# Other cost figures in the planner that orders the side work of a one-core decoder block

## The chip, the cores and the metric

The kernel runs on one core of a Trainium2 chip. Its time is the device time of one execution in microseconds (us); the figure given is the median of several. The core has five engines that each take their own instructions in order: TensorE (PE, matrix multiplication), VectorE (DVE), ScalarE (ACT), GpSimd (POOL) and SyncE (SP), which here only issues transfers.

## The reference

One layer of a hybrid decoder block on 256 rows of width 2048, all in float32. A normed input goes through one wide projection (17 slices); three branches mix the rows (a gated linear recurrence, sparse attention with compressed, selected and window keys, and attention with a forget bias); each is gated, projected, scaled by a merge gate and summed; an output projection, and an embedding that is gated by another projection, are added.

```python
hn = rms_norm(h, ln_gain[l])
z = split_columns(hn @ w_in[l] + b_in[l])
y_a = rglru_branch(z['lru_x'], ...) * jax.nn.silu(z['lru_gate'])
...
y_b = nsa_branch(q_b, k_c, v_c, k_s, v_s, k_w, v_w, g_b) * jax.nn.silu(z['nsa_gate'])
y_c = fox_branch(...) * jax.nn.silu(z['fox_gate'])
merged = (mg[:, :, 0] * (y_a @ w_branch[l, 0])
          + mg[:, :, 1] * (y_b @ w_branch[l, 1])
          + mg[:, :, 2] * (y_c @ w_branch[l, 2]))
h = h + merged @ w_out[l]
e = rms_norm(p[l] @ w_ple[l], ple_gain[l])
h = h + jax.nn.sigmoid(h @ w_ple_gate[l]) * e
```

## The kernel before, in words

**Main work.** All weights are one stream of 384 pieces of up to 128 x 1024 values ("halves" in the code; called pieces here). SP loads a piece into one of six `raw` tiles. ACT rounds it to the fast matmul type (`wh<-raw`), DVE subtracts to get the remainder (`wl<-raw,wh`), and PE multiplies with both: three matmuls of 128x512 for each product, so that the result is near float32. A usual piece has two rows of 128 weights and two row blocks (t) of the output, which makes 12 matmuls. `wh` and `wl` each have four buffers (`AHEAD`+1, line 1391): the rounding of a piece waits until PE is done with the piece four places earlier. Results grow in `main0` to `main3`, two at a time, in turns.

**The order of the stream.** Input slices first, among them `nsa_gate`; then for each of the three branches b and four column groups j one `merge` group (eight pieces, the merge gate) and one `proj` group (four pieces, the branch's projection); then output and embedding gate. "Proj 0" below is the first projection of branch A; "merge 0" is the group ahead of it, and "merge 1" the one behind. Proj 0 reads `yh` and `yl`, the two parts of branch A's gated output `yl` (the name `k_yl` stands for both the branch output and the low part).

**Side work.** Everything else is written as generators that are advanced a step at a time between the pieces: `lru_task` (line 741; four of them, lru0 to lru3, two channel tiles each, of branch A: convolution, gates, a scan into `yl`), `nsa_task` (line 922; eight, of branch B: scores in a `bank`, a maximum, an exponential with row sums, scaling, a turn through a transposition and DMAs, the product with V), `fox_task` (branch C), `norm_rows`, `turn_chunk` and so on. `y_split` (line 1102) waits for all four lru tasks; it multiplies by the gate (`k_yl<-k_yl,k_gl`), rounds (`k_yh<-k_yl` on ACT) and subtracts (`k_yl<-k_yl,k_yh` on DVE), in four steps of two channel tiles.

**What sets the order.** While the program is built, a planner keeps a clock for each engine. Each recorded instruction passes through `Metered.run` (line 207; all instructions therefore carry line 208 in the profile), which adds an estimated cost to its engine's clock; `Clock.add` lets it start only after what it reads. `Side.tick` (line 257) is called once or twice a piece and advances up to three waiting tasks in turn, but returns as soon as the later of the DVE and ACT clocks is more than `LIMITS` (2.5 to 3.5 us, line 1404) ahead of PE's clock. Urgent tasks (`turn_chunk`, `norm_rows`, `y_split`) are advanced ahead of the others. `settle`, `powers` and `landed` hold a task until PE's clock has passed a moment, so that PE's small matmuls stand behind enough main work. `need` (line 1281) is the other end: where a piece cannot be written until a task is done (each `proj` piece needs one step of `y_split`), it advances tasks without regard to the limit until it is:

```python
for name in wait:
    n = 0
    while name not in side.done:
        ...
        clock.t["pe"] += 200.0
        side.tick(True)
```

These clocks exist only while the program is built. On the chip each engine simply runs its list, with semaphores.

## Time and profile before

| | |
|---|---|
| median of 3 runs | 1060.82 us (1060.35 to 1060.99) |
| profiled execution, its time | 1061.77 us |
| its span from first to last instruction | 1060.0 us |
| PE busy | 1053.3 us, 99% of the span |
| PE weight loads busy | 879.3 us, 83% |
| DVE busy | 772.2 us, 73% |
| ACT busy | 620.6 us, 59% |
| DMA moved | 237.52 MB, mean 224 GB/s |

### The profile page before, as it was taken

What the parts mean: (1) busy time and instruction counts of PE and PEld (TensorE: products, weight loads), DVE (VectorE), ACT (ScalarE), POOL (GpSimd) and SP (SyncE); (2) the same over time, 40 slices, a digit from 0 to 9 for tenths busy, and PEclk for the clock granted to TensorE, in tenths of its full rate; (3) what the DMA queues carried; (4) which work ended last, traced back from release to release, by engine and by line L of the source; (5) the groups of instructions that cost most, each with busy time, mean ns of one, the idle gap of its engine ahead of it and who ended that gap; (6) DMA issues with size and microseconds to landing.
All of it is one profiled execution on the core that took longest, in us unless ns stands there. A gap on an engine that the chain in (4) does not pass through costs nothing.

```text
span 1060.0 us, 14061 instructions
## 1 busy us (share of the span) xinstructions
PE 1053.3 (99%) x4903; PEld 879.3 (83%) x4903; DVE 772.2 (73%) x1151; ACT 620.6 (59%) x940; POOL 53.1 (5%) x77
## 2 busy tenths in 40 slices
PE   9999999999999999999999999999999999999998
PEld 7888889888888888888888888888888888888886
DVE  7777889897778678678987965555766566766664
ACT  7668877768766667544645644555555444444442
POOL 0000001110000000020110000000001000000000
PEclk9999999999999999999999999999999999999999
DMA  9767868787657467577677566766676877778751
GB/s 337 248 201 260 257 200 280 233 266 226 217 189 218 150 198 216 182 234 251 194 235 239 186 222 207 223 213 214 219 244 196 264 235 220 236 250 257 278 207 60
DMA packets 86295, 237.52 MB, mean 224 GB/s; under 512 B 14024, under 2 KB 31312, under 8 KB 86224
## 3 DMA queue, kind: packets, MB, share of 16 engines
q1 hardware_dynamic: 81504, 220.87, 64.8%
q0 software_dynamic: 4720, 15.76, 5.5%
q8 instruction: 38, 0.62, 0.3%
q14 instruction: 33, 0.27, 0.1%
HBM read 215.61 MB, written 4.20 MB: 207 GB/s over the span
## 4 chain that ended last, share of the span: by engine, by line
PE 91%; DVE 3%; DMA 2%; ACT 2%; SPq 1%; issue 1%; DVEq 0%; ACTq 0%
PE main L208 87%; PE bank L208 4%; SPq L208 1%; DVE wl L208 1%; DMA raw<-in_w 1%; DMA k_fpz<-k_fprob 1%; DMA k_pz<-k_prob 1%; ACT wh L208 0%; ACT k_pz L208 0%; DVE k_fq L208 0%; DVE k_prob L208 0%; DVE k_fprob L208 0%; DVE k_pt L208 0%; DVE k_fbias L208 0%; DVE k_fx L208 0%
## 5 line engine op out<-in xcount | busy, mean ns | idle before, releaser
L208 DVE TENSOR_TENSOR wl<-raw,wh 128x1024 fp32r<-128x1024 f32 (+2 forms) x388 | 459.8, 1197 | 186.0 <-ACT wh L208 185.2
L208 ACT ACTIVATE wh<-raw 128x1024 fp32r<-128x1024 f32 (+2 forms) x388 | 400.2, 1040 | 318.3 <-PE main L208 281.3
L208 PE MATMUL main<-wh,k_hnh 128*128 128x512 f32 (+2 forms) x1026 | 395.0, 385 | 0.5 <-ACT wh L208 0.5
L208 PE MATMUL main<-wh,k_hnl 128*128 128x512 f32 (+1 forms) x1024 | 393.0, 384 | 0.0
L208 PE MATMUL main<-wl,k_hnh 128*128 128x512 f32 (+2 forms) x1026 | 392.9, 384 | 0.0
L208 PEld LDWEIGHTS main<-wh,k_hnh 128*128 128x128 f32 x1026 | 193.2, 189 | 37.5 <-ACT wh L208 1.1
L208 PEld LDWEIGHTS main<-wh,k_hnl 128*128 128x128 f32 x1024 | 192.5, 188 | 38.1
L208 PEld LDWEIGHTS main<-wl,k_hnh 128*128 128x128 f32 x1026 | 193.2, 189 | 35.9 <-DVE wl L208 0.2
L208 PE MATMUL main<-wl,k_yh 128*128 128x512 f32 x192 | 74.9, 390 | 0.1
L208 PE MATMUL main<-wh,k_yh 128*128 128x512 f32 x192 | 74.9, 390 | 0.0
L208 PE MATMUL main<-wh,k_yl 128*128 128x512 f32 x192 | 74.8, 389 | 0.0
L208 PE MATMUL main<-wh,k_mth 128*128 128x512 f32 x128 | 49.8, 389 | 0.0
L208 PE MATMUL main<-wl,k_mth 128*128 128x512 f32 x128 | 49.8, 389 | 0.0
L208 PE MATMUL main<-wh,k_mtl 128*128 128x512 f32 x128 | 49.8, 389 | 0.0
L208 PE MATMUL main<-wh,k_hth 128*128 128x512 f32 x128 | 49.8, 389 | 0.0
L208 PE MATMUL main<-wl,k_hth 128*128 128x512 f32 x128 | 49.8, 389 | 0.0
L208 PE MATMUL main<-wh,k_htl 128*128 128x512 f32 x128 | 49.8, 389 | 0.0
L208 PEld LDWEIGHTS main<-wl,k_yh 128*128 128x128 f32 x192 | 36.0, 188 | 7.7 <-DVE wl L208 0.5
L208 PEld LDWEIGHTS main<-wh,k_yl 128*128 128x128 f32 x192 | 36.0, 188 | 7.5
L208 PEld LDWEIGHTS main<-wh,k_yh 128*128 128x128 f32 x192 | 36.1, 188 | 7.4
L208 ACT ACTIVATE k_mg<-k_mg 128x512 f32<-128x512 f32 x24 | 15.2, 633 | 26.6 <-DVE k_mg L208 26.3
L208 PEld LDWEIGHTS main<-wl,k_mth 128*128 128x128 f32 x128 | 24.0, 188 | 5.0
(243 smaller groups left out, 948.4 us busy)
## 6 DMA issues: line engine op xcount, KB each, us to landing
raw<-in_w SPq DMA_DIRECT2D x369, 512.0 KB, 4.5
bias<-in_b_in POOLq DMA_DIRECT2D x21, 256.0 KB, 5.2
raw<-in_w SPq DMA_DIRECT2D x8, 408.0 KB, 4.0
k_pz<-k_prob SPq DMA_DIRECT2D x16, 128.0 KB, 4.2
e_dram<-k_e POOLq DMA_DIRECT2D x4, 512.0 KB, 3.6
k_merged<-k_zt SPq DMA_DIRECT2D x16, 128.0 KB, 3.2
k_xc<-in_x POOLq DMA_DIRECT2D x4, 512.0 KB, 6.4
k_hx<-k_zt SPq DMA_DIRECT2D x16, 128.0 KB, 3.6
```

The costliest lines, as they stand in the source:

```text
L208: r = call(out, *args, **kw)
```

## The change

The planner's estimates for three kinds of instruction become larger; no tile, no instruction and no limit is changed by hand.

```diff
                 cost = 185.0 + 93.0 * columns + 0.833 * n + (1280.0 if tables != clock.tables else 0.0)
+                if "accum_out" in kw and n >= P:
+                    cost += n
                 clock.tables = tables
             elif which == "v":
-                cost = 150.0 + 1.05 * n
+                if name == "tensor_reduce":
+                    n = 1
+                    for m in ins[0].shape[1:]:
+                        n *= m
+                spaced = any(x.ap[-1][0] != 1 and x.shape[-1] > 1 for x in [out] + ins)
+                cost = 150.0 + (1.7 if spaced or name == "tensor_tensor_scan" else 1.05) * n
```

So an ACT instruction that also sums its rows is charged one nanosecond more for each element of a row, a DVE row reduction is charged by what it reads in place of what it writes, and DVE instructions with an operand whose elements do not lie side by side, and scans, are charged 1.7 ns an element in place of 1.05.

With other estimates the planner writes the same instructions in another order: each engine has as many as before, ACT changes its function table nine times in both, and the lists of PE, DVE and ACT part where the first lru tasks begin, in the first input slices. Three places are shown here, around the start of proj 0.

**DVE, the last scan of branch A (`k_yl<-k_lru`, the end of lru3).** Before, it stands among the remainders (`wl`) of merge 0's early pieces, and the gated products follow long after:

```order
L208 SCALAR_TENSOR_TENSOR k_lru_2527<-k_uc_2209,k_lru_2527 128x512
L208 TENSOR_TENSOR k_lru_2527<-k_lru_2527,k_lru_2526 128x512
L208 TENSOR_TENSOR wl_2606<-raw_2490,wh_2605 128x1024
L208 TENSOR_TENSOR wl_2630<-raw_2532,wh_2629 128x1024
L208 SCALAR_TENSOR_TENSOR k_yl_567<-k_lru_2525,k_lru_2527 128x256 x2
L208 TENSOR_TENSOR wl_2648<-raw_2559,wh_2647 128x1024
```

Now it stands behind the two `k_mg<-main` rows, which read merge 0's finished result, and the first gated product (`k_gl`) and its low part (`k_yh`) come a softmax later:

```order
L208 SCALAR_TENSOR_TENSOR k_mg_2953<-main_85,rsr,bias_2814 128x512
L208 SCALAR_TENSOR_TENSOR k_mg_2954<-main_86,rsr,bias_2814 128x512
L208 SCALAR_TENSOR_TENSOR k_yl_567<-k_lru_2699,k_lru_2701 128x256 x2
L208 ISA sp_pc_2742,sp_m_2740<-bank_87,cst 128x16
L208 ISA k_prob_2744,sp_m_2740<-bank_88,cst 128x256
L208 ISA k_prob_2744,sp_m_2740<-bank_87,cst 128x256
L208 TENSOR_SCALAR sp_sm_2729<-sp_sm_2729 128x6
L208 SCALAR_TENSOR_TENSOR k_pc_472_2731<-sp_pc_2730,sp_sm_2729,k_pc_472_2731 128x2x16
L208 STREAM_TRANSPOSE k_prob_2732<-k_pz_2733 128x512
L208 TENSOR_TENSOR k_ql_2994<-k_qn_2101,k_qh_2993 128x256
L208 TENSOR_TENSOR k_yl_567<-k_yl_567,k_gl_982 128x512
L208 TENSOR_TENSOR k_yl_2998<-k_yl_567,k_yh_2997 128x512
```

(Of the softmax the rows that repeat are left out: six ISA rows in all, a reciprocal and a product on `sp_sm`, a second `k_pc` and two pairs of `k_pz` scalings.)

**ACT at the same place, now.** Between merge 0's tanh (`k_mg`) and the first `k_yh` stand a rounding of a weight piece, the exponentials of two heads, their `k_pc` parts and the next query's `k_qh`:

```order
L208 ACTIVATE wh_2934<-raw_2841 128x1024
L208 ACTIVATE k_mg_2953<-k_mg_2953 128x512
L208 ACTIVATE k_mg_2954<-k_mg_2954 128x512
L208 ACTIVATE wh_2961<-raw_2862 128x1024
L208 ACTIVATE sp_pc_2730,sp_sm_2729<-sp_pc_2730,sp_m_2728 128x16
L208 ACTIVATE k_pz_2733,sp_sm_2729<-k_prob_2732,sp_m_2728 128x4x32 x2
L208 ACTIVATE k_pc_472_2731<-sp_pc_2730,sp_sm_2729 128x2x16 x2
L208 ACTIVATE sp_pc_2742,sp_sm_2741<-sp_pc_2742,sp_m_2740 128x16
L208 ACTIVATE k_pz_2745,sp_sm_2741<-k_prob_2744,sp_m_2740 128x4x2x32 x2
L208 ACTIVATE k_qh_2993<-k_qn_2101 128x256
L208 ACTIVATE k_yh_2997<-k_yl_567 128x512
```

**PE, the seam between merge 0 (`main_86<-...k_hnl`) and proj 0 (`main_83<-wh,k_yh`).** Before, one follows the other:

```order
L208 MATMUL main_86<-wl_2842,k_hnh_130 128x512
L208 MATMUL main_86<-wh_2841,k_hnl_131 128x512
L208 MATMUL main_83<-wh_2859,k_yh_2768 128x512
L208 MATMUL main_83<-wl_2860,k_yh_2768 128x512
L208 MATMUL main_83<-wh_2859,k_yl_2769 128x512
```

Now six score matmuls of an nsa task (`bank<-kk`) stand between; twelve more of them stand further up in the list and six inside proj 0, where before the first twelve stood inside proj 0's last piece:

```order
L208 MATMUL main_86<-wl_2865,k_hnh_130 128x512
L208 MATMUL main_86<-wh_2864,k_hnl_131 128x512
L208 MATMUL bank_87<-kk,k_qh_2695 128x272 x2
L208 MATMUL bank_87<-kk,k_ql_2696 128x272
L208 MATMUL bank_88<-kk,k_qh_2695 128x256 x2
L208 MATMUL bank_88<-kk,k_ql_2696 128x256
L208 MATMUL main_83<-wh_2890,k_yh_2997 128x512
L208 MATMUL main_83<-wl_2891,k_yh_2997 128x512
L208 MATMUL main_83<-wh_2890,k_yl_2998 128x512
```

## The prediction

> **What bounds the kernel now.** I read the page's busy times first, then who PE waited for, then the chain that ended last.

> ```profile
> span 1060.0 us, 14061 instructions
> PE 1053.3 (99%) x4903; PEld 879.3 (83%) x4903; DVE 772.2 (73%) x1151; ACT 620.6 (59%) x940; POOL 53.1 (5%) x77
> ```

> ```profile
> PE bank L208 <- PEq L1473: 0.8, 1, 0.8
> PE main L208 <- ACT wh L208: 0.5, 1, 0.5
> PE bank L208 <- DVE k_fpt L208: 0.2, 1, 0.2
> ```

> ```profile
> 312.42 0.73 PE bank L208 x6
> ...
> 617.00 438.03 PE main L208 x1932
> ```

> PE is the bound from end to end. Its list of waits has three entries, 1.5 us together, and the longest two belong to the start. From the chain of waits I take two lines: its longest stretch is 1932 matmuls in 438.03 us, 0.227 us each, with nothing between; the other shows six small matmuls of the side work in 0.73, 0.12 each. A new order leaves the number of matmuls as it is, so it can save at most those 1.5 us, 0.14%. It can lose any amount, if PE comes to a matmul whose operand is late. So the question is only where PE now has to wait, and every wait of PE is paid in full.

> The tightest place is where a projection needs a branch's output. In the profile of before, the seam between merge 0 and proj 0 reads like this; the first fence is PE's timeline, the second DVE's, the third ACT's.

> ```profile
> 269.94 0.39 PE L208 MATMUL main<-wh,k_hnh 128*128 128x512 f32 x1
> ...
> 294.19 0.39 PE L208 MATMUL main<-wh,k_hnl 128*128 128x512 f32 x1
> 294.42 0.39 PE L208 MATMUL main<-wh,k_yh 128*128 128x512 f32 x1
> ```

> ```profile
> 262.95 1.27 DVE L208 TENSOR_TENSOR_SCAN k_yl<-k_lru,k_lru 128x256 f32<-128x256 f32 x2
> 276.64 0.68 DVE L208 TENSOR_TENSOR k_yl<-k_yl,k_gl 128x512 f32<-128x512 f32 x1
> 278.03 0.69 DVE L208 TENSOR_TENSOR k_yl<-k_yl,k_yh 128x512 fp32r<-128x512 f32 x1 [0.70 <-ACT k_yh L208]
> 294.77 0.69 DVE L208 TENSOR_TENSOR k_yl<-k_yl,k_yh 128x512 fp32r<-128x512 f32 x1 [0.70 <-ACT k_yh L208]
> 296.52 1.40 DVE L208 SCALAR_TENSOR_TENSOR k_mg<-main,rsr,bias 128x512 f32<-128x512 f32 x2
> ```

> ```profile
> 270.13 1.06 ACT L208 ACTIVATE wh<-raw 128x1024 fp32r<-128x1024 f32 x1 [0.95 <-PE main L208]
> ...
> 277.36 0.63 ACT L208 ACTIVATE k_yh<-k_yl 128x512 fp32r<-128x512 f32 x1 [2.26 <-DVE k_yl L208]
> ```

> Proj 0 begins at 294.42, 0.23 us behind merge 0's last matmul. The last scan of branch A was started 31.5 us earlier and the first low part 16.4 us earlier; the fourth, at 294.77, is needed by proj 0's last piece only. That lead is what the change spends.

> **The change part by part.** The new figures are nearer to the trace: a scan of 256 was charged 150 + 1.05 x 256 = 419 ns and is now 585, a scaling of 512 with spaced operands was 688 and is now 1020.

> ```profile
> L208 DVE TENSOR_TENSOR_SCAN k_yl<-k_lru,k_lru 128x256 f32<-128x256 f32 x8 | 5.1, 676 | 0.0
> L208 DVE TENSOR_TENSOR k_qn<-k_z,sp_nss 128x512 f32<-128x512 f32 x4 | 4.1, 1065 | 0.0
> ```

> But nothing runs faster for it. The planner lets side tasks go only while its DVE and ACT clocks are less than 2.5 to 3.5 us ahead of PE's; dearer steps fill that sooner, urgent tasks are served first, and what is left over is the lru tasks, which take turns with others. So lru3 slips from 31 us ahead of proj 0 to behind merge 0's end, and is finished only because proj 0 demands it. In the order shown, the last scan stands behind `k_mg<-main_86`, which reads merge 0's finished sum. On an engine that runs its list in order, that scan cannot start before PE has ended merge 0; and PE's next matmul but six needs what the scan leads to. The wait is thus built in, and I work it out as a chain from T, the moment at which PE could begin proj 0. The rows for it are the softmax of before, first DVE's, then ACT's:

> ```profile
> 308.52 0.17 DVE L208 CUSTOM_DVE_ANT_0 sp_pc<-bank,cst 128x16 f32<-128x16 f32 x1
> 309.31 1.22 DVE L208 TENSOR_TENSOR wl<-raw,wh 128x1024 fp32r<-128x1024 f32 x1
> 313.73 0.17 DVE L208 TENSOR_SCALAR sp_sm<-sp_sm 128x6 f32<-128x6 f32 x1
> 314.77 0.25 DVE L208 SCALAR_TENSOR_TENSOR k_pc<-sp_pc,sp_sm,k_pc 128x32 fp32r<-128x32 f32 x1 [0.45 <-ACT k_pc L208]
> 315.50 0.48 DVE L208 TENSOR_SCALAR k_pz<-k_pz,sp_sm 128x128 f32<-128x128 f32 x2
> 316.24 0.42 DVE L208 TENSOR_TENSOR k_ql<-k_qn,k_qh 128x256 fp32r<-128x256 f32 x1 [0.27 <-ACT k_qh L208]
> 317.36 0.71 DVE L208 STREAM_TRANSPOSE k_prob<-k_pz 128x512 f32<-128x512 f32 x1
> 319.10 0.16 DVE L208 TENSOR_SCALAR sp_sm<-sp_sm 128x6 f32<-128x6 f32 x1
> 321.46 1.22 DVE L208 TENSOR_TENSOR wl<-raw,wh 128x1024 fp32r<-128x1024 f32 x1
> 323.11 1.24 DVE L208 STREAM_TRANSPOSE k_prob<-k_pz 128x1024 f32<-128x1024 f32 x1
> ```

> ```profile
> 308.22 0.31 ACT L208 ACTIVATE sp_pc<-sp_pc,sp_m 128x16 f32<-128x16 f32 x1 [0.15 <-DVE sp_m L208]
> 308.52 0.51 ACT L208 ACTIVATE k_pz<-k_prob,sp_m 128x128 f32<-128x128 f32 x1
> 309.54 0.30 ACT L208 ACTIVATE sp_pc<-sp_pc,sp_m 128x16 f32<-128x16 f32 x1
> 309.83 0.76 ACT L208 ACTIVATE k_pz<-k_prob,sp_m 128x256 f32<-128x256 f32 x1
> 311.33 1.05 ACT L208 ACTIVATE wh<-raw 128x1024 fp32r<-128x1024 f32 x1
> 314.42 0.53 ACT L208 ACTIVATE k_pc<-sp_pc,sp_sm 128x32 fp32r<-128x32 f32 x2 [0.72 <-DVE sp_sm L208]
> 315.81 0.40 ACT L208 ACTIVATE k_qh<-k_qn 128x256 fp32r<-128x256 f32 x1
> ```

> *First wait.* (1) The two `k_mg` rows, 0.70 each. The second needs merge 0's last matmul. Ahead of the first stands the remainder of a piece whose rounding is let go by the start of merge 0's last piece (as at 269.94, where PE starts a piece and ACT's rounding follows at 270.13), so at T - 2.5; behind the gate products and the softmax maximum that share DVE there, I put the pair's end at T + 1.7; the earliest is T + 1.2. (2) The two scans, 1.2: T + 2.9. (3) The maxima of one head, 308.52 to 309.31, 0.8: T + 3.7; their scores, six matmuls, run on PE meanwhile. (4) DVE now needs row sums from ACT, which has to do the second tanh (its `k_mg` is done at T + 1.7; some 0.55), a rounding (0.95), and one head's exponentials (308.22 to 309.54, 1.3): T + 4.5, with the handover 4.6. (5) From the sums to the last scaling pair: 313.73 to 315.50 is 1.77, and 0.4 for the pair: T + 6.8, then the transposition, 0.6: T + 7.4. (6) ACT meanwhile: two `k_pc` from 314.42 (0.69 behind 313.73) and 0.45 long, T + 5.75; the second head's exponentials, 309.54 to 311.33, 1.8, T + 7.55; `k_qh` 0.4, T + 7.95. This is later than DVE's 7.4, so DVE's `k_ql` runs from T + 8.0 to 8.35. (7) Gate product, rounding, low part: 276.64 to 278.03 and 0.69, 2.1 in all: T + 10.4. PE's first two matmuls need `yh` alone (T + 9.7), the third needs the low part; a handover of 0.1 later it starts at T + 10.5, as if proj 0 had begun at T + 10.05. The six score matmuls (as the six small ones above, 0.75) have run in that time and are no loss. **9.3 us.**

> *Second wait.* Proj 0's first piece is done at T + 12.8 (12 x 0.227). Its second needs the second part of `yl`. DVE, free at T + 10.35, first scales the other head, 319.10 to 321.46, 2.36, and then takes 2.1: T + 14.8. The piece begins in effect at T + 14.45: **1.7 us**. *Third.* It holds the other six score matmuls and ends at T + 17.9. The third part follows a remainder (1.14) and 2.1 after T + 14.7, at T + 17.95: just in time. The fourth follows a transposition of 1024 (1.16) and a remainder (1.14): T + 22.25, where PE is ready at T + 20.65. The last piece begins in effect at T + 21.9: **1.3 us**.

> Behind proj 0 the next remainders are ready (one was made at T + 20.2, and PE needs it at T + 24.6), and the nsa tasks run further ahead than before, since DVE and ACT worked while PE stood. The DMAs that move with them (16 turns of `k_pz` on SP, the `wd` load of lru3 on POOL) do not set the end: the landing of a turn is read only behind proj 0's rounding of later pieces, and SP's weight loads run six pieces ahead and gain time while PE stands. ACT's nine table loads stay. Sum: 9.3 + 1.7 + 1.3 = **12.3 us**, against savings of 0.2 (the one wait that is not at the start).

> *Bounds.* Below: with ACT never the limit, step 4 to 6 shrink to DVE's own rows (T + 1.2 + 1.2 + 0.8, then 1.04 to `k_pc`, 0.7 and 0.4 of scalings, 0.6, 0.35) and 2.1: T + 8.4, 7.2 us for the first wait and about 9 in all. Above: were ACT a full piece late (its rounding and four gate activations that stand there, each about as long as `k_qh`: 0.95 + 4 x 0.4), 2.6 more, 15.

> *The clock.* A wait of 9 us is longer than anything in the trace of before, except its start, where PE's matmuls are slow:

> ```profile
> 8.11 0.63 PE L208 MATMUL main<-wl,k_hnh 128*128 128x512 f32 x1
> 8.54 0.63 PE L208 MATMUL main<-wh,k_hnl 128*128 128x512 f32 x1
> ...
> 9.33 0.39 PE L208 MATMUL main<-wl,k_hnh 128*128 128x512 f32 x1
> 9.56 0.40 PE L208 MATMUL main<-wh,k_hnl 128*128 128x512 f32 x1
> ```

> The first two starts are 0.43 us apart, the last two 0.23. If that clock came back behind the wait, the first piece would take 5.1 in place of 2.7 us and end at T + 14.8: just when the second part arrives, so 1.7 of wait turns into slow work at no cost. If it lasted as long as at the start (up to about 9 us into the span), the second piece would lose another 2.3 and absorb the 1.3 of the third wait: +1.0 in all. I leave it out of the sum and in the range.
> [...]

> **The rivals.** *Cover after all:* the scan comes late in DVE's list, but waits in the list need not be waits in time, if ACT and DVE have slack. For it: ACT is 59% busy. Against it: the `k_mg` row reads merge 0's last matmul, and the rows behind it add up to 8.4 us even at their shortest. What remains is that the second and third waits vanish: 6 to 9 us, about 1068. *More than one place:* the order differs everywhere, and the eight nsa and eight fox tasks must end before proj 4 and proj 8; one of them late by a softmax, as here, adds 3 to 6: 1076 to 1079. For it: the same softmax rows stand in each of them. Against: behind proj 0 the nsa tasks are ahead, not behind. *Not slower:* the planner with truer clocks places each small matmul later than its operand, PE's 0.2 us goes, and proj 0's wait is covered. It would take the chain from `k_mg` to the first low part to be at most the 0.75 us of score matmuls and the 2.1 us that a measurement could not tell; it is 8.4 at the least. 1060.6.

> **How the numbers follow.** Forecast 12.3: the profiled time would go from 1061.77 to 1074.0; the profiled execution lies 0.9 us above the median of the runs shown, so the median goes from 1060.82 to 1073.1. Forecast (10 to 15 us, with or without the slow clock) 0.72; cover 0.13; more places 0.12; not slower 0.03. The range takes the forecast's own, 1071 to 1076, out to most of the two neighbours: 1068 to 1077.5. A measurement of this kernel tells about 0.2%, 2.1 us, from no change: slower 0.96, within 0.03, faster 0.01 (more than 1.5 us is not there to be saved).

> **What would show it.** The profile after should have one long wait of PE, some 9 us, ahead of the first `main<-wh,k_yh`, released by ACT `k_yh` or DVE `k_yl`, near 297 us (294.4 and 18 score matmuls, 2.3), and two of 1 to 2 us in the next 15; DVE's scans right behind `k_mg`; and from the fox groups on the same rows as before, 12 us later. Matmuls 0.43 apart behind the wait would be the slow clock. I am wrong if PE's waits stay at 1.5 us, or if a wait of several us stands elsewhere.

## The result and the profile after

| | before | after |
|---|---|---|
| median of the runs | 1060.90 us (4 runs, 1060.35 to 1062.33) | 1072.51 us (4 runs, 1072.46 to 1072.62) |
| ratio | | 1.0106, 95% interval 1.0091 to 1.0121 |
| span of the profiled execution | 1060.0 us | 1070.7 us |
| mean granted TensorE clock | 0.999 | 0.993 |

The change made the kernel 11.6 us slower; 1073.1 was forecast, with a range of 1068 to 1077.5.

The page of the kernel after, its busy times and its row of the granted clock:

```profile
PE 1054.2 (98%) x4903; PEld 879.9 (82%) x4903; DVE 772.7 (72%) x1151; ACT 619.6 (58%) x940; POOL 52.8 (5%) x77
...
PEclk9999999999979999999999999999999999999999
```

Every engine has as many instructions as before and is busy for as long, to within 1 us. Only the order differs. New is the 7 in the clock's row: in the slice from 294 to 321 us TensorE did not run at full speed throughout. Now whom PE waited for, after:

```profile
PE main L208 <- ACT k_yh L208: 9.7, 1, 9.7
PE main L208 <- ACT wh L208: 0.8, 2, 0.5
PE bank L208 <- PEq L1480: 0.8, 1, 0.8
PE main L208 <- DVE wl L208: 0.2, 1, 0.2
```

One wait of 9.7 us has come in, and of the two that were forecast behind it the list has nothing; the three small entries all lie in the first 12 us. PE's timeline around proj 0 shows why:

```profile
295.11 0.39 PE L208 MATMUL main<-wh,k_hnl 128*128 128x512 f32 x1
295.34 0.41 PE L208 MATMUL bank<-kk,k_qh 128*128 128x272 f32 x2
...
295.94 0.28 PE L208 MATMUL bank<-kk,k_ql 128*128 128x256 f32 x1
305.90 0.80 PE L208 MATMUL main<-wh,k_yh 128*128 128x512 f32 x1 [9.67 <-ACT k_yh L208]
...
310.75 0.63 PE L208 MATMUL main<-wh,k_yl 128*128 128x512 f32 x1
311.18 0.63 PE L208 MATMUL main<-wh,k_yh 128*128 128x512 f32 x1
...
311.94 0.39 PE L208 MATMUL main<-wh,k_yl 128*128 128x512 f32 x1
312.17 0.40 PE L208 MATMUL main<-wh,k_yh 128*128 128x512 f32 x1
...
320.56 0.40 PE L208 MATMUL main<-wh,k_yl 128*128 128x512 f32 x1
```

T, the moment at which PE could begin proj 0, is 295.34 here. The matmuls at 310.75 and 311.18 start 0.43 us apart, those at 311.94 and 312.17 0.23: behind the wait the granted clock is 0.50 (from 298.17 to 311.82 us), and the matmuls lie as far apart as at the start of before (0.43 from 8.11 to 8.54). The first piece lasts from 305.90 to 311.18, 5.28 us in place of 2.72. Proj 0 ends at 320.56 + 0.23 = 320.79. Its 48 matmuls at 0.227 and twelve small score matmuls (six ahead of it in 0.75, six inside it in 0.74) would have ended it at T + 12.4 = 307.7. So **13.1 us** were lost here.

DVE and ACT at the same place, after:

```profile
293.75 1.23 DVE L208 TENSOR_TENSOR wl<-raw,wh 128x1024 fp32r<-128x1024 f32 x1 [0.52 <-ACT wh L208]
...
295.41 1.22 DVE L208 TENSOR_TENSOR wl<-raw,wh 128x1024 fp32r<-128x1024 f32 x1
296.55 1.40 DVE L208 SCALAR_TENSOR_TENSOR k_mg<-main,rsr,bias 128x512 f32<-128x512 f32 x2
297.87 1.26 DVE L208 TENSOR_TENSOR_SCAN k_yl<-k_lru,k_lru 128x256 f32<-128x256 f32 x2
299.05 0.15 DVE L208 CUSTOM_DVE_ANT_0 sp_pc<-bank,cst 128x16 f32<-128x16 f32 x1
...
300.89 0.17 DVE L208 TENSOR_SCALAR sp_sm<-sp_sm 128x6 f32<-128x6 f32 x1 [1.00 <-ACT k_pz L208]
...
303.11 0.71 DVE L208 STREAM_TRANSPOSE k_prob<-k_pz 128x512 f32<-128x512 f32 x1
304.15 0.42 DVE L208 TENSOR_TENSOR k_ql<-k_qn,k_qh 128x256 fp32r<-128x256 f32 x1 [0.33 <-ACT k_qh L208]
304.50 0.68 DVE L208 TENSOR_TENSOR k_yl<-k_yl,k_gl 128x512 f32<-128x512 f32 x1
305.88 0.69 DVE L208 TENSOR_TENSOR k_yl<-k_yl,k_yh 128x512 fp32r<-128x512 f32 x1 [0.69 <-ACT k_yh L208]
```

```profile
292.68 1.99 ACT L208 ACTIVATE wh<-raw 128x1024 fp32r<-128x1024 f32 x2
297.33 1.29 ACT L208 ACTIVATE k_mg<-k_mg 128x512 f32<-128x512 f32 x2 [2.66 <-DVE k_mg L208]
...
305.21 0.63 ACT L208 ACTIVATE k_yh<-k_yl 128x512 fp32r<-128x512 f32 x1 [1.09 <-DVE k_yl L208]
```

This is the chain of the forecast, row for row: merge-gate pair, scans, softmax, query part, gated product, rounding, low part. Of the 8 us from the scans to the first low part DVE is idle for 2.0 in the three gaps shown, and for 0.4 in one more, each time for ACT.

Behind proj 0 the kernel after is a little better than before. The same stretch of each profile by the clock, 322 to 460 and 460 to 650 us, of before and then of after (columns: length, then busy time and count of PE, PEld, DVE, ACT, POOL, the granted clock, the DMA share, GB/s):

```profile
322.00:460.00 138.00, 137.77 (x667) 115.59 (x666) 104.63 (x218) 88.55 (x178) 7.57 (x10) 1.00 0.64 197
460.00:650.00 190.00, 189.76 (x866) 157.55 (x865) 149.77 (x253) 100.43 (x157) 13.67 (x19) 1.00 0.72 223
```

```profile
322.00:460.00 138.00, 138.00 (x672) 116.65 (x671) 103.22 (x208) 86.38 (x175) 3.32 (x9) 1.00 0.62 196
460.00:650.00 190.00, 190.00 (x869) 158.07 (x868) 150.54 (x256) 101.40 (x159) 18.48 (x21) 1.00 0.71 221
```

After, PE started 5 and 3 matmuls more in the same time. The mixture of shapes in a stretch is not quite the same, so I also added up, over each stretch, what the times between two starts exceed the usual distance of their kind (0.227 us for a main matmul): 2.46 and 1.78 before, 1.37 and 1.30 after, 1.6 us less in all. (The level depends on what is taken for the usual distance of the small matmuls: with the median of each kind over all runs it is 1.91 and 1.54 before, 0.71 and 1.08 after. The difference, then 1.7, hardly does.) Thus 13.0 more at proj 0 (13.1 against 0.13), less 1.6: 11.4, where the medians differ by 11.6. (The spans differ by 10.7, since the profiled execution of before lay 0.9 above the median of its runs.)

### The profile page after: what moved, and what is told of

Same layout as the page of the kernel before. It is cut to its first block, busy times and chain, and to the rows that moved or that the text cites. A ratio compares the mean times of both kernels' runs of the same rounds, so it can differ in the third digit from the quotient of the medians.

```text
span 1070.7 us, 14059 instructions
## 1 busy us (share of the span) xinstructions
PE 1054.2 (98%) x4903; PEld 879.9 (82%) x4903; DVE 772.7 (72%) x1151; ACT 619.6 (58%) x940; POOL 52.8 (5%) x77
## 4 chain that ended last, share of the span: by engine, by line
PE 97%; ACT 1%; DVE 1%; DMA 0%; issue 0%; SPq 0%; DVEq 0%
PE main L208 93%; PE bank L208 5%; DMA raw<-in_w 0%; ACT wh L208 0%; ACT k_pz L208 0%; DVE wl L208 0%; SPq L208 0%; DVE k_fin L208 0%; ACT k_gn L208 0%; DVE k_mg L208 0%; ACT k_th L208 0%; ACT k_yh L208 0%; DVE k_yl L208 0%; ACT sp_pc L208 0%; DVE sp_sm L208 0%
## 5 line engine op out<-in xcount | busy, mean ns | idle before, releaser
L208 DVE TENSOR_TENSOR wl<-raw,wh 128x1024 fp32r<-128x1024 f32 (+2 forms) x388 | 460.6, 1198 | 191.9 <-ACT wh L208 189.3
L208 ACT ACTIVATE wh<-raw 128x1024 fp32r<-128x1024 f32 (+2 forms) x388 | 401.3, 1041 | 337.6 <-PE main L208 302.2
L208 PE MATMUL main<-wh,k_hnh 128*128 128x512 f32 (+2 forms) x1026 | 394.4, 385 | 0.9 <-ACT wh L208 0.8
L208 PE MATMUL main<-wl,k_hnh 128*128 128x512 f32 (+2 forms) x1026 | 392.3, 383 | 0.2 <-DVE wl L208 0.2
L208 PE MATMUL main<-wh,k_hnl 128*128 128x512 f32 (+1 forms) x1024 | 392.3, 383 | 0.0
L208 PEld LDWEIGHTS main<-wh,k_hnh 128*128 128x128 f32 x1026 | 192.7, 188 | 38.3 <-ACT wh L208 1.8
L208 PEld LDWEIGHTS main<-wh,k_hnl 128*128 128x128 f32 x1024 | 192.2, 188 | 38.0
L208 PEld LDWEIGHTS main<-wl,k_hnh 128*128 128x128 f32 x1026 | 192.5, 188 | 36.4 <-DVE wl L208 0.5
L208 PE MATMUL main<-wh,k_yh 128*128 128x512 f32 x192 | 76.5, 398 | 9.7 <-ACT k_yh L208 9.7
L208 PE MATMUL main<-wh,k_yl 128*128 128x512 f32 x192 | 75.9, 395 | 0.0
L208 PE MATMUL main<-wl,k_yh 128*128 128x512 f32 x192 | 75.9, 395 | 0.0
L208 PEld LDWEIGHTS main<-wh,k_yh 128*128 128x128 f32 x192 | 36.7, 191 | 17.4 <-ACT k_yh L208 10.1
L208 PE MATMUL main<-wh,k_mth 128*128 128x512 f32 x128 | 49.8, 389 | 0.0
L208 PE MATMUL main<-wl,k_mth 128*128 128x512 f32 x128 | 49.8, 389 | 0.0
L208 PE MATMUL main<-wh,k_mtl 128*128 128x512 f32 x128 | 49.8, 389 | 0.0
L208 PE MATMUL main<-wh,k_hth 128*128 128x512 f32 x128 | 49.8, 389 | 0.0
L208 PE MATMUL main<-wl,k_hth 128*128 128x512 f32 x128 | 49.8, 389 | 0.0
L208 PE MATMUL main<-wh,k_htl 128*128 128x512 f32 x128 | 49.8, 389 | 0.0
L208 PEld LDWEIGHTS main<-wh,k_yl 128*128 128x128 f32 x192 | 36.7, 191 | 8.4 <-DVE k_yl L208 0.7
L208 PEld LDWEIGHTS main<-wl,k_yh 128*128 128x128 f32 x192 | 36.8, 192 | 7.4
L208 ACT ACTIVATE k_mg<-k_mg 128x512 f32<-128x512 f32 x24 | 15.2, 632 | 24.8 <-DVE k_mg L208 24.5
L208 PEld LDWEIGHTS main<-wh,k_mth 128*128 128x128 f32 x128 | 24.0, 188 | 5.0
```

The costliest lines, as they stand in the source:

```text
L208: r = call(out, *args, **kw)
```

## The experiments

Each median stands beside that of the kernel before on the same chip in the same session: 1061.44 for the first four, 1061.59 for the four single figures, 1061.79 for the last two. "Lost at proj 0" is the sum over the time between starts from 293 to 322 us as above; before loses 0.13 there, after 13.1. The two theories are those of the expectations: the *place* (a scan and gated products behind the merge-gate pair of merge 0 make the loss, there alone) and the *spread* (the new order costs in other places, or through other work).

| run | built on | median us | ratio to before, 95% | PE's wait at proj 0 | lost at proj 0 |
|---|---|---|---|---|---|
| e4_late_in_before | before | 1070.11 | 1.0076 (1.0060 to 1.0092) | 7.1 | 9.7 |
| e2_forced_alone | after | 1067.33 | 1.0050 (1.0032 to 1.0069) | 4.9 | 6.6 |
| e1_nsa_after_lru | after | 1066.15 | 1.0040 (1.0027 to 1.0053) | 3.7 | 6.7 |
| e3_keep_busy | after | 1072.47 | 1.0097 (1.0082 to 1.0113) | 2.3 in three | 4.0 and the 40 matmuls (9.1) |
| e5_row_sums_alone | before | 1060.09 | 0.9985 (0.9976 to 0.9994) | none | 0.04 |
| e6_reduce_alone | before | 1068.37 | 1.0064 (1.0049 to 1.0079) | 5.8 | 8.1 |
| e7_spaced_alone | before | 1066.67 | 1.0048 (1.0031 to 1.0065) | 4.4 | 7.7 |
| e8_scan_alone | before | 1066.16 | 1.0043 (1.0028 to 1.0058) | 2.1 | 3.9 |
| e9_lru_let_ahead | after | 1062.27 | 1.0005 (0.9996 to 1.0014) | none | 0.08 |
| e10_row_sums_lru_first | before | 1058.74 | 0.9975 (0.9964 to 0.9985) | none | 0.09 |

**The place without the figures (e4).** The kernel before, old figures, with lru3's scans held back until proj 0 demands them:

```diff
+        while i == 3 and "forced" not in st:
+            yield False
         for c in range(2):
...
                 assert n < 2000, name
+                if name == "ysplit00":
+                    st["forced"] = True
                 clock.t["pe"] += 200.0
```

> The kernel before, with its old cost figures, but lru3 holds its last scan back until proj 0 asks for it. The scan then stands right behind the k_mg pair, a transposition of 1024, a k_ql and the product chain behind it. Place theory: k_mg pair's end T + 2.0 to 2.5, then 1.2, 1.2, 0.35 and 2.1: about 6.4 us lost, and 2.6 for the clock if it falls: 1067.3 without, 1069.9 with it, and no other wait over 1 us. Spread theory (it is the figures, not this one place): within 2 us of before, 1059 to 1063.

Measured 1070.11. DVE's and then PE's timeline of this run:

```profile
297.55 1.40 DVE L208 SCALAR_TENSOR_TENSOR k_mg<-main,rsr,bias 128x512 f32<-128x512 f32 x2
298.87 1.26 DVE L208 TENSOR_TENSOR_SCAN k_yl<-k_lru,k_lru 128x256 f32<-128x256 f32 x2
```

```profile
302.89 0.79 PE L208 MATMUL main<-wh,k_yh 128*128 128x512 f32 x1 [7.14 <-ACT k_yh L208]
```

The pair ends at 298.87, 3.3 us behind PE's readiness at 295.60, some 0.8 later than the expectation had it. The scans behind the pair are enough for a loss of 9.7 of the 13.1 us; no new figure is needed for it.

**The figures without the place (e9).** The reverse: the kernel after, all figures in, but the lru tasks may run 1.5 us further ahead of PE:

```diff
-                if self.clock.behind() > LIMITS["q0" in self.done][group is self.active] and not hurry:
+                if self.clock.behind() > LIMITS["q0" in self.done][group is self.active] + 1500.0 * task[0].startswith("lru") and not hurry:
                     return
```

> The kernel after with all its new figures, and one thing more: a task whose name begins with lru may still be advanced while the planner's DVE and ACT clocks are up to 1.5 us further ahead of PE's than the usual limit. In the order that results, the scans of branch A stand far ahead of the merge-gate pair of merge 0 again, and all four gated products with their low parts stand ahead of it too (the last of them some 23 rows ahead in DVE's list). Place theory (the loss is made by what stands behind the merge-gate pair ahead of proj 0 and by nothing else in the new order): no wait of PE at proj 0, the granted clock stays full, and what the new figures saved between 322 and 650 us (1.6 us) stays: 1059 to 1061 us, ratio to before 0.998 to 1.000. Rival (the new figures cost time in other places as well, or the loss comes from the changed order of the softmax work): a wait of several us stays or turns up elsewhere, 1064 to 1072 us. If 1061 to 1063 comes out, the key rows that a piece still has to force cost PE a wait of 1 to 2 us, which the list of waits must then show.

Measured 1062.27, above the place theory's 1059 to 1061 and within what the text gave for waits of 1 to 2 us. At proj 0 nothing is lost (0.08), the clock stays at 0.999, and what was saved behind it stays (1.34 and 1.30). But PE waits earlier, twice; here are its timeline and ACT's at the first of the two waits:

```profile
141.51 0.45 PE L208 MATMUL main<-wh,k_hnh 128*128 128x512 f32 x1
142.72 0.50 PE L208 MATMUL main<-wl,k_hnh 128*128 128x512 f32 x1 [0.76 <-DVE wl L208]
```

```profile
137.46 1.28 ACT L208 ACT_TABLE_LOAD   x1
138.76 0.51 ACT L208 ACTIVATE k_th<-k_zt,vec 128x256 f32<-128x256 f32 x1
...
140.37 3.72 ACT L208 ACTIVATE wh<-raw 128x1024 fp32r<-128x1024 f32 x4
```

From 137.46 to 140.37 ACT is taken by a table load and four gate activations of a task, and PE's next piece stands behind them: 142.72 - 141.51 is 0.98 more than a matmul's distance. PE loses 1.03 in the same way at 180, where ACT's rounding stands behind activations of an lru task. The two make 2.0 of the 3.0 us that PE loses more than before between 12 and 293 us. I had expected the cost, if any, at the key rows; as I read these rows, it is the price of the wider limit itself, though no run shows that apart. So at proj 0 the spread theory falls, and the limit that the tasks ran into seems to protect something: it keeps ACT's roundings on time.

**How long the chain is (e2).** In after, steps that proj 0 demands advance lru and `y_split` alone, so the softmax leaves the chain:

```diff
             for task in list(group):
+                if hurry and not task[0].startswith(("lru", "ysplit")):
+                    continue
```

> The changed kernel, but when proj 0 forces branch A's output, only the lru tasks and y_split are advanced, not the nsa tasks. The last scan stays behind the k_mg pair; the softmax rows between it and the gated products go behind them. Chain theory: k_mg pair's end at T + 2.5 as measured, scans 1.2, product to low part 2.1: PE has its third matmul at T + 5.9 and has lost 4.7 us, with no second or third wait. With an idle time of 4.3 us the clock may or may not fall; if it does as in the changed kernel (13 matmuls, 0.2 us each) another 2.6, now with no wait to hide under. 1064.2 without, 1066.8 with it. If the softmax rows in between did not matter: 1072.

Measured 1067.33, with a wait of 4.9 us. Half the wait was the softmax that was forced along with the scans; the rest is the pair, the scans and the product. The half clock cost 1.5 us in the profiled execution (6.6 lost, 5.1 of it the wait from start to start), where the expectation had 2.6 for it.

**lru before nsa (e1), a miss.** In after, the nsa tasks wait for lru3 too:

```diff
-        yield from side.wait(f"q{g}", "kks", "vs0", "vs1", "cmpend", "vec")
+        yield from side.wait(f"q{g}", "kks", "vs0", "vs1", "cmpend", "vec", "lru3")
```

> The changed kernel, but the nsa tasks begin only when lru3 is done, so that lru3 has the planner's steps to itself; all new cost figures stay. In its order the last scan stands some eight pieces ahead of proj 0, two of the four gated products ahead of the k_mg pair, the other two two remainders behind it. Place theory (the loss is lru3's place alone): no wait of PE over 0.5 us at proj 0; the third part is ready about T + 6.9 at the latest, where PE wants it at T + 5.9, so at most 1 us there. Since the changed kernel lost some 13 us at proj 0 and won 1.6 elsewhere, 1059.5 us, between 1059 and 1061. Spread theory (the new figures make a worse order everywhere): still over 1066.

Measured 1066.15, not 1059.5. The scans are early now, but the last two gated products still stand behind the pair; DVE's and then ACT's timeline:

```profile
297.80 1.40 DVE L208 SCALAR_TENSOR_TENSOR k_mg<-main,rsr,bias 128x512 f32<-128x512 f32 x2
300.85 2.36 DVE L208 TENSOR_TENSOR wl<-raw,wh 128x1024 fp32r<-128x1024 f32 x2 [1.65 <-ACT wh L208]
303.13 0.68 DVE L208 TENSOR_TENSOR k_yl<-k_yl,k_gl 128x512 f32<-128x512 f32 x1
```

```profile
298.58 1.29 ACT L208 ACTIVATE k_mg<-k_mg 128x512 f32<-128x512 f32 x2 [2.56 <-DVE k_mg L208]
299.77 2.94 ACT L208 ACTIVATE wh<-raw 128x1024 fp32r<-128x1024 f32 x3
```

This is a second thing at the seam that the expectation's chain did not contain. ACT's list has the two `k_mg` tanh ahead of the next roundings, so ACT stands idle for DVE's pair (2.56), and then DVE for ACT's rounding (1.65). Whatever follows a remainder behind the pair is late by that much more, though neither engine is full. PE's third piece waited 3.7 us and then ran its first 11 matmuls at half clock, 2.2 us more.

**The clock by itself (e3).** In after, 40 matmuls whose product is overwritten by proj 0's first, put ahead of proj 0:

```diff
+        if h["kind"] == "proj" and h["key"] == 0 and h["first"]:
+            for _ in range(40):
+                nc.tensor.matmul(out[0], hn[0][0][:, 0, :P], h["wh"][:, 0, :], start=True, stop=True)
```

> The changed kernel, with 40 matmuls of no use (128x512, into the accumulator that proj 0 then begins anew, from tiles that are ready) ahead of proj 0's first, 9.1 us that lie in the 9.7 us of waiting. PE's clock should stay full. My theory: the low clock behind the wait cost next to nothing, since the second and third waits come out in its place (low part at T + 11.3, second part T + 15.6, fourth T + 23); end of proj 0 within 0.3 us, so 1072.2 us, between 1071.7 and 1072.8. Clock theory: 13 matmuls at 0.43 in place of 0.23 us cost their 2.6 us: 1069.9.

Measured 1072.47 against 1072.51 of after (ratios to before 1.0097 and 1.0106, each in its own session). PE's timeline where the added work stands, and its list of waits:

```profile
295.74 9.25 PE L475 MATMUL main<-wh,k_hnh 128*128 128x512 f32 x40
...
305.57 0.50 PE L208 MATMUL main<-wh,k_yh 128*128 128x512 f32 x1 [0.58 <-ACT k_yh L208]
```

```profile
PE main L208 <- ACT k_yh L208: 2.3, 3, 1.1
```

The clock was full (1.000). With that the second and third wait of the forecast appear: start to start, PE stands 0.74 at the first piece, 1.23 at the second and 0.79 at the fourth. In after these two waits are filled by the slow matmuls. Both kernels lose 13.1 us at proj 0 (here 4.0 and the 9.1 of the added work), so here the half clock costs nothing of its own.

**One figure at a time (e5 to e8).** Each is the kernel before with one of the figures; the four expectations stand behind the edits in the same order, e5 to e8:

```diff
+                if "accum_out" in kw and n >= P:                      (e5)
+                    cost += n
...
+                if name == "tensor_reduce":                           (e6)
+                    n = 1
+                    for m in ins[0].shape[1:]:
+                        n *= m
...
+                cost = 150.0 + (1.7 if spaced else 1.05) * n                          (e7)
...
+                cost = 150.0 + (1.7 if name == "tensor_tensor_scan" else 1.05) * n    (e8)
```

> Of the three new figures only the one for ACT's exponentials and squares with row sums. In this order the last scan stands ten pieces ahead of proj 0 and all four gated products ahead of the k_mg pair. Place theory: no new wait of PE; as before, 1060 to 1061.5. If the figure for sums carried the loss: over 1065.

> Only the new figure for DVE's row reductions. In this order the last scan stands one remainder ahead of the k_mg pair, and the gated products behind that pair and two heads' maxima. Place theory: k_mg pair's end T + 2.5, maxima 1.0, product to low part 2.1: low part at T + 5.7, PE loses 4.5 there (0.8 of the wait is filled by score matmuls), then 1.3 ahead of the second piece and 0.4 at the third: some 6 us, 1065.5 to 1068.5.

> Only the new figure for DVE instructions with spaced operands. In this order the last scan stands eight pieces ahead of proj 0, the first gated product ahead of the k_mg pair, the second a remainder behind it. Place theory: no wait at the first piece; the second part is there at T + 5.7 and PE wants it at T + 3.2: 2.6 us, then up to 0.5 at the last: 1062.5 to 1064.5, less up to 1.6 that the truer clock saved elsewhere in the changed kernel.

> Only the new figure for scans. In this order two gated products stand ahead of the k_mg pair, the third two remainders behind it. Place theory: the third part is there at T + 6.9 and PE wants it at T + 5.9: about 1 us, 1060.5 to 1062.5.

The row sums on ACT alone made no wait, and 1060.09 is slightly faster than before. Each of the three figures on DVE alone delays proj 0 by several us. e6 came out at the upper end of what was expected; e7 and e8 were missed by 2 and 4 us, for the same reason as e1. Their products stand behind the pair and a remainder, and I had left out the idle time for ACT; in e7 DVE's timeline reads

```profile
297.74 1.40 DVE L208 SCALAR_TENSOR_TENSOR k_mg<-main,rsr,bias 128x512 f32<-128x512 f32 x2
300.79 1.23 DVE L208 TENSOR_TENSOR wl<-raw,wh 128x1024 fp32r<-128x1024 f32 x1 [1.64 <-ACT wh L208]
```

and both then paid for slow matmuls (12 in e7, 7 in e8), which I had not counted on behind waits this short. The losses at proj 0 do not add up (8.1 + 7.7 + 3.9 against 13.1): how far DVE's list slips matters, and any of the three already carries it past the pair.

**The best of what was seen (e10).** The kernel before, the row-sum figure alone, and lru tasks first among those that take turns:

```diff
+                if "accum_out" in kw and n >= P:
+                    cost += n
...
-            for task in list(group):
+            for task in sorted(group, key=lambda x: group is self.active and not x[0].startswith("lru")):
```

> The kernel before with the new figure for row sums alone (which, alone, came to 0.9985 of before) and one thing more: of the waiting tasks the lru tasks are advanced first, ahead of the nsa tasks that take turns with them. All four gated products of branch A then stand ahead of the merge-gate pair of merge 0. Place theory: the start of proj 0 loses nothing, as with the row-sum figure alone, so being earlier still is worth nothing there; 1059.0 to 1060.5 us, ratio 0.998 to 0.9995. Rival (an earlier branch A shortens the run as well, since the work behind it moves forward): 1057 to 1058.5 us. Other rival (the nsa tasks that now come later are themselves awaited): a wait of PE at proj 4's group of 1 to 4 us, 1061 to 1064 us.

Measured 1058.74 in eight runs, ratio 0.9975 (0.9964 to 0.9985): faster than before and than after. The time lies a little below the place theory's 1059.0 to 1060.5 and a little above the first rival's 1057 to 1058.5, and the interval reaches into both, so the run does not decide between them; the other rival's wait at proj 4 did not come. Its span is 1057.5, the longest entry in PE's list of waits, at the start of the program, is

```profile
PE main L208 <- ACT wh L208: 0.8, 2, 0.7
```

and from 322 to 650 us PE exceeds the ideal by 2.55 in place of 4.24, 1.7 less. The spans of the two profiled executions differ by 2.5; another 1.0 of that lies in the first 12 us, where PE's excess is 4.7 in before, 3.7 here, and between 3.3 and 4.1 in the other kernels. How much of the 3.05 us between the medians is owed to the order and how much to such a start is open. Whether serving lru first adds anything to the row-sum figure is open: e5's interval (0.9976 to 0.9994) and e10's overlap.

## Why the prediction was right, step by step

*The place* was right: the only new wait of PE behind the first 12 us is ahead of the first `main<-wh,k_yh`, released by ACT's `k_yh`, at 296 us where "near 297" stood. e4 makes it with the old figures, and e9 unmakes it with the new.

*First wait.* Forecast 9.3, of which 9.1 ahead of the first matmul and 0.2 at the third; PE's list shows 9.7 ahead of the first, which is 9.8 from start to start, and nothing at the third. The steps, as times behind T = 295.34:

| step | forecast | measured |
|---|---|---|
| (1) end of the `k_mg` pair | T + 1.7 | T + 2.5 |
| (2) scans | T + 2.9 | T + 3.7 |
| (4) row sums from ACT | T + 4.6 | T + 5.55 |
| (5) last scaling | T + 6.8 | T + 7.8 |
| (6) `k_ql` | T + 8.35 | T + 9.15 |
| (7) low part | T + 10.4 | T + 11.15 |
| first `yh` ready | T + 9.7 | T + 10.5 |

The only term that was mis-sized by more than 0.2 is step (1): I put one remainder ahead of the pair, let go at T - 2.5, and by the rows at 293.75 and 295.41 there were two behind a pair of roundings, the second started at T + 0.07. That is 0.8 late; every later step keeps this distance to within 0.2. ACT was the limit in steps (4) and (6), as forecast: DVE's rows there are `[1.00 <-ACT k_pz L208]` and `[0.33 <-ACT k_qh L208]`.

*Second and third wait, and the clock.* The form was wrong, the sum nearly right. The prediction had 1.7 and 1.3 of waiting in the sum and the half clock only in the range, "0 to +1.0". The half clock came, and the first piece took 2.56 us more, which covered the second wait and most of the third; some 0.3 is left at 317.7. It stood for 5.9 us of work (305.90 to 311.82), a little past the first piece: of the prediction's two cases the shorter one, at no cost, and not the longer one at +1.0. e3, without the half clock, has 1.23 and 0.79 of waiting there and the same time. So the argument that slow work would hide under the second wait held, and so did its cost of nothing. By the forecast's own steps proj 0 ends at T + 24.6; measured is T + 25.45, all of it the 0.8 of step (1). The loss is 13.1 for 12.3.

*Savings.* "It can save at most those 1.5 us" was wrong as a bound, and the 0.2 that the sum is set against is not taken off in the forecast of 1073.1, which is 1060.82 + 12.3. 1.6 us were saved between 322 and 650, where the list of before has 0.2 in all, and e10 is 3.05 us faster than before. The step that failed is the reading of PE's list of waits as the whole of its idle time. A matmul's modelled duration (0.39) is longer than the distance to the next (0.227), so a gap shorter than the difference, 0.16, is not seen, and a longer one shows by that much too short. An example of before, from its PE timeline:

```profile
541.31 0.39 PE L208 MATMUL main<-wh,k_hnl 128*128 128x512 f32 x1
541.93 0.50 PE L208 MATMUL bank<-k_fpt,k_fx 128*128 128x512 f32 x1 [0.24 <-DVE k_fpt L208]
```

The list has 0.24; start to start it is 0.62 - 0.227 = 0.39. With three more such gaps, 0.24 at 371.9, 0.17 at 405.0 and 0.31 at 405.8, each behind DVE, this makes 1.1 of the 1.6 us; after has no gap over 0.15 there. The two errors, 0.8 too little lost and 1.6 too little saved, have opposite signs and leave the forecast loss 0.7 us too high: that the time came out this close is in part luck.

*The rivals.* Cover after all: e3 shows both later waits, so they were not covered. More than one place: behind proj 0 nothing got worse. Not slower: fell with the first wait. What I had not listed is that the three DVE figures each suffice (e6 to e8).

## What to carry to other kernels

A cost model that sets an order is judged by the order it makes, not by how true its figures are: here truer figures, those for DVE, used up a fixed allowance sooner, and the task that was served last fell behind an instruction that reads the end of the stage. Look for the first instruction in an engine's list that waits for the stage's last result, and see what stands behind it that the next stage needs: that, with the idle time of a second engine that waits for the same result, is the price. And read lost time of an engine whose instructions overlap (PE's matmuls here are 0.39 us long and 0.227 apart) from start to start, not from the list of waits alone.

## What the runs showed of the hardware

In after the granted clock is 0.50 from 298.17 to 311.82 us, 13.65 us, and 1.00 just ahead of it and behind it; PE's wait of 9.67 us ends within it, at 305.90. Here are the windows of after, then those of e1 (PE's wait 3.65, ending at 304.53) and of e6 (5.75, ending at 301.98); the third number from the end of a row is the mean granted clock:

```profile
294.63:298.04 3.41, 1.59 (x10) 1.24 (x8) 3.41 (x11) 0.72 (x3) 0.00 (x0) 1.00 0.79 240
298.04:301.45 3.41, 0.00 (x0) 0.00 (x0) 2.35 (x11) 2.82 (x8) 0.86 (x2) 0.52 0.71 226
301.45:304.86 3.41, 0.00 (x0) 0.00 (x0) 2.65 (x10) 2.60 (x9) 0.00 (x0) 0.50 0.01 5
304.86:308.27 3.41, 2.37 (x6) 1.87 (x7) 2.26 (x9) 1.16 (x3) 0.00 (x0) 0.50 0.35 77
308.27:311.68 3.41, 3.41 (x10) 2.67 (x9) 2.71 (x6) 0.89 (x2) 0.00 (x0) 0.50 0.00 0
```

```profile
299.25:302.66 3.41, 1.62 (x13) 1.42 (x11) 1.81 (x2) 3.41 (x4) 0.85 (x2) 1.00 0.68 207
302.66:309.49 6.83, 4.96 (x12) 3.86 (x13) 5.44 (x18) 1.31 (x3) 0.00 (x0) 0.51 0.52 160
```

```profile
294.60:298.01 3.41, 1.62 (x10) 1.26 (x9) 3.41 (x6) 0.14 (x1) 0.00 (x0) 1.00 0.77 271
298.01:301.42 3.41, 0.00 (x0) 0.00 (x0) 2.39 (x14) 3.38 (x10) 1.36 (x4) 1.00 0.72 244
301.42:304.83 3.41, 2.85 (x7) 2.23 (x8) 2.42 (x11) 2.15 (x8) 0.00 (x0) 0.52 0.06 23
```

In after the clock stayed at 0.50 through the window with 2.37 us of PE's work and through the next, with 3.41. In the first row of e1 and of e6 PE is busy for 1.62 of 3.41 us alike (busy times go by the modelled ends of matmuls). In e1 the mean clock of the next 6.83 us is 0.51; in e6 it is 1.00 in the next 3.41 us, in which PE did nothing, and 0.52 in the 3.41 behind them. These rows do not show what decided between the two.

A longer wait did not always bring more slow work: behind the 2.1 us of e8 seven matmuls were slow, 0.2 us each, behind the 3.65 of e1 eleven, behind the 4.44 of e7 twelve, and behind the 4.91 of e2 six of 128x512. In e3, whose waits are 1.23 us at most, the clock stayed full (1.000). So in these runs the slow work behind a wait was a part of its price that its length did not tell.
